# Recurrence layer: one dense v per step, key products over half the rows each, PSUM banks by chunk parity

## The chip, the cores and the metric
The kernel runs on one core of one Trainium2 chip. The metric is the device time of one execution in microseconds, the median of several runs. Engines are named as in the profile: PE is TensorE, ACT ScalarE, DVE VectorE, POOL GpSimd, SP the queue that issues most transfers.

## The reference
Two layers of a backbone over 256 latent and 256 context tokens of width 1024. Layer 0 is a state-space layer, layer 1 a chunked gated delta rule, and each is followed by an MLP. The change lies in the recurrence of layer 1: 16 heads, head dimension 128, chunks of 64 tokens, two directions, first over the four chunks of the context and then over the four of the latents. For every chunk and direction it computes

```python
v_new = u_i - einsum('bhcd,bhde->bhce', w_i, state)
new_state = state * exp(glast_i)[..., None, None] + einsum('bhcd,bhce->bhde', kend_i, v_new)
o_i = einsum('bhcd,bhde->bhce', qg_i, state) + einsum('bhcs,bhse->bhce', intra_i, v_new)
```

`u_i` and `w_i` come from a triangular inverse of a 64 x 64 matrix per chunk, head and direction. The outputs of the latents are normalised per head, gated, and multiplied by `w_out`.

## The kernel before
All projections, the MLPs and the readout are products of weights and activations that are split in a high and a low part, three products each. The recurrence layer runs in `gdn_phase` as a set of tasks: projections (`gdn_proj`, tile `proj`), convolutions (`conv_silu`), inverses (`gdn_t`, tiles `ap`, `up`, `ep`, `wp`), chains (`gdn_chain`), normalisation (`gdn_read`, `ot`) and the product with `w_out` (`gdn_out`, `wo`). `drive` steps through the tasks with a clock of its own, `Clock`, which estimates each instruction; the order of the program follows from it and from the scheduler of the tile framework. Each engine then runs its instructions in the fixed order, waiting on semaphores.

A chain is one head. Its two directions run side by side in one tile: at step n direction 0 works on chunk n and direction 1 on chunk 3-n or 11-n. The two chunks have different parity, so one has partitions 0 to 63 and the other 64 to 127 (`rows`). Eight steps make a chain, and at most NCH = 3 chains run at a time, in slots x = 0, 1, 2. A step consists of
- `ks`: keys x state, one product of 128 rows and 64 columns of the array per direction (in the profile `c<-S,kt`)
- `r0` on VectorE: values minus decay times `ks` (`r<-c,neg,vs`)
- `ub`: the inverse x `r0`, one 64 x 64 product per direction, written over `ks` (`c<-r,ub`, in the first step `c<-vs,ub`)
- `v2` on ScalarE: that product scaled per token (`v<-c,vsc`); from step 4 on also `vn`, its plain copy (`vn<-c`), and before it `qs`, queries x state
- `kv`: `v2` x keys (`c<-v,kn`), then the new state `S` on VectorE, one instruction per direction
- from step 4 on `op`: intra-chunk weights x `vn`, added to the output `oa`

Before, `v2` is two blocks of 128 columns, one per direction. In each block the other direction's 64 rows stay at the zeros that `gdn_zero` wrote once, so one full-array product gives both states:

```python
for d in range(2):
    nc.scalar.activation(v2[rows[d], d], vp[rows[d]], AF.Identity, scale=...)
kvw = self.cb[x][:, 128:384]
mm(kvw, kn[:, ms], v2.rearrange("p d e -> p (d e)"))
```

Each chain has a PSUM bank of its own, `cb[x]` (tiles `c0`, `c1`, `c2`): `ks` in columns 0 to 127 and the two states in 128 to 383.

Of the kernel before, what the change touches and what calls it, by code (L numbers as in the profile page):

```python
# [8 lines left out]
F32 = mybir.dt.float32  # L9
# [3 lines left out]
AF = mybir.ActivationFunctionType  # L13
# [1407 lines left out]
NPR, NT, NQK, NCH, NHI, NRB, LZ = 1, 2, 4, 3, 2, 3, 2  # L1421
# [36 lines left out]
class K3(K2):  # L1458
# [3 lines left out]
    def gdn_init(self, pool):  # L1462

        nc, V, G = self.nc, self.nc.vector, self.nc.gpsimd
        P = self.g = pool
        c2 = self.c2 = P.tile([128, NCONST2], F32, name="c2")
        nc.sync.dma_start(c2, self.I["consts2"])
        self.cw = P.tile([128, 32, 5], F32, name="cw")
        nc.sync.dma_start(self.cw, self.I["conv"])
        self.onh = P.tile([128, 1], F32, name="on")  # L1470
        nc.sync.dma_start(self.onh, self.I["onorm"])
        self.pp, self.npp = [], 0
        for n in range(2):
            t = P.tile([128, 524], F32, name=f"pp{n}")
            self.pin(G.memset(t, 0.0))
            self.pp.append(t)
        self.id16 = P.tile([128, 64], F16, name="id16")
        self.pin(G.tensor_copy(self.id16, c2[:, M_ID:M_ID + 64]))
        self.idm2 = P.tile([128, 128], F16, name="idm2")
        self.pin(G.tensor_scalar(self.idm2, self.ident, -2.0, None, op0=OP.mult))  # L1480
        self.id1k = P.tile([128, 64], F32, name="id1k")
        self.pin(G.tensor_scalar(self.id1k, c2[:, M_ID:M_ID + 64], 1024.0, None, op0=OP.mult))
        V.tensor_scalar(self.cw, self.cw, 0.5, None, op0=OP.mult)
        V.tensor_scalar(self.onh, self.onh, 0.5, None, op0=OP.mult)
        self.nb, self.lo = [], []
        for n in range(2):
            for L, name in ((self.nb, "nb"), (self.lo, "lo")):
                L.append(P.tile([128, 8, 128], F16, name=f"{name}{n}"))
        self.cb = [self.bank(f"c{n}", f"c{n}", bufs=1) for n in range(3)]

        self.cp = [(b[:, 0:128], b[:, 128:256], b[:, 256:384]) for b in self.cb] + [tuple(b[:, 384:512] for b in self.cb)]
        self.nhi, self.loeng = NHI, (G, V)
        self.wslot, self.hslot, self.wq = Slots(4), Slots(NHI), []
        self.cslot, self.fslot = Slots(2), Slots(2)
        self.pslots, self.nproj = [Slots(NPR), Slots(1)], 0
        self.oslot = [Slots(1) for _ in range(NCH)]
        self.v2 = []
        for x in range(NCH):
            self.v2.append([P.tile([128, 2, 128], F32, name=f"v2{x}{n}") for n in range(2)])

    def swapped(self, x, h, d, n):

# [334 lines left out]
    def gdn_chain(self, p, h2, st):  # L1837

        nc, V = self.nc, self.nc.vector
        W = self.gw  # L1840
        kt, qt, kn, vs = st["kt"], st["qt"], st["kn"], st["vs", h2]
        x = (2 * p + h2) % NCH
        ks, *kv = self.cp[x]
        vp = ks
        hd = 2 * p + h2
        col = lambda x, n: x[:, n, hd:hd + 1]
        new = lambda name, shape, bufs=1: W.tile(shape, F32, name=f"{name}{x}", bufs=bufs)
        mm = lambda o, l, r: nc.tensor.matmul(o, l, r, start=True, stop=True, skip_group_check=True)
        S = None
        for n in range(8):  # L1850
            cs = (n, 3 - n if n < 4 else 11 - n)
            rows = [slice(64 * (c % 2), 64 * (c % 2) + 64) for c in cs]
            ms, lat = MS[n], n >= 4
            if S is None:
                r0 = vs[:, ms]
            else:
                for d in range(2):
                    mm(ks[rows[d]], kt[:, cs[d]], S[:, d])
                r0 = new("r0", [128, 128])
                V.scalar_tensor_tensor(r0, ks, col(self.neg, n), vs[:, ms], op0=OP.mult, op1=OP.add)  # L1860
                if lat:
                    qs = self.tr("qs")[:, 0:128]
                    for d in range(2):
                        mm(qs[rows[d]], qt[:, cs[d] - 4], S[:, d])
                yield
            for d in range(2):
                mm(vp[rows[d]], st["ub", d][rows[d], cs[d] // 2, h2], r0[rows[d]])
            if n < 7:
                v2 = self.v2[x][n % 2]
                for d in range(2):  # L1870
                    nc.scalar.activation(v2[rows[d], d], vp[rows[d]], AF.Identity, scale=self.vsc[rows[d], n, hd:hd + 1])
            if n == 4:
                yield from self.oslot[x].take()
                oacc = st["o", h2] = new("oa", [128, 2, 128])
            if lat:
                oa = oacc[:, ms - 2]
                if n < 6:
                    nc.scalar.activation(oa, qs, AF.Identity, scale=col(self.egs, n))
                else:
                    V.scalar_tensor_tensor(oa, qs, col(self.egs, n), oa, op0=OP.mult, op1=OP.add)  # L1880
                vn = new("vn", [128, 128])
                nc.scalar.copy(vn, vp)
            yield
            if n < 7:
                if x < 3:
                    kvw = self.cb[x][:, 128:384]
                    mm(kvw, kn[:, ms], v2.rearrange("p d e -> p (d e)"))
                else:
                    for d in range(2):
                        mm(kv[d], kn[:, ms], v2[:, d])  # L1890
                Sn = new("S", [128, 2, 128], 2)
                if S is None:
                    if x < 3:
                        nc.scalar.copy(Sn.rearrange("p d e -> p (d e)"), kvw)
                    else:
                        for d in range(2):
                            nc.scalar.copy(Sn[:, d], kv[d])
                else:
                    for d in range(2):
                        V.scalar_tensor_tensor(Sn[:, d], S[:, d], self.egl[:, n, d, hd:hd + 1], kv[d],  # L1900
                                               op0=OP.mult, op1=OP.add)
                S = Sn
                yield
            if lat:
                op = self.tr("op")[:, 0:128]
                for d in range(2):
                    mm(op[rows[d]], st["ibd", d][rows[d], cs[d] // 2 - 2, h2], vn[rows[d]])
                V.tensor_tensor(oa, oa, op, op=OP.add)
                yield
# [130 lines left out]

    def gdn_zero(self):

        for t in self.nb + self.lo + [t for v in self.v2 for t in v]:
            self.pin(self.nc.gpsimd.memset(t, 0.0))
            yield

# [215 lines left out]
```

## Time and profile before
| | us |
|---|---|
| runs | 1623.61, 1618.85, 1622.08 |
| median | 1622.08 |
| the profiled execution | 1624.46 |
| its span, first to last instruction | 1622.7 |

| engine | busy us | share | instructions |
|---|---|---|---|
| PE | 1469.8 | 91% | 12370 |
| DVE | 1096.8 | 68% | 2036 |
| ACT | 776.3 | 48% | 1635 |
| POOL | 650.6 | 40% | 590 |

TensorE's clock as granted is 0.947 of full over the span. The recurrence layer runs from about 755 to 1420 us: projections alone at first, chains from 900 us on, the last projection at 1332 us, the last chain's end at about 1397 us, and the rest of `w_out` after it. An fp32 product is two matmul records in the profile, so 224 records of `c<-v,kn` are 112 products.

### The profile page before, as it was taken

The numbers are of one execution on the slowest core, as the hardware profiler recorded it, in microseconds if no ns is written. First come the engines' busy times: TensorE is split into PE (matmuls) and PEld (weight loads), VectorE is DVE, ScalarE is ACT, GpSimd is POOL, SyncE is SP. The second block draws the span as 40 slices with busy tenths as digits, with TensorE's granted clock in tenths as the row PEclk, the third lists the DMA queues.
The fourth block names the chain that finished last, engine by engine and source line by source line (L and its number), as shares of the span: only waits on it lengthen the run. The fifth ranks groups of instructions, "written<-read, shape, count | busy, mean of one in ns | idle before, by whom it ended". The sixth has DMA issues, their size and how long they took to land. (4 is left out here: it accounts for less than half of the span.)

```text
span 1622.7 us, 31318 instructions
## 1 busy us (share of the span) xinstructions
PE 1469.8 (91%) x12370; PEld 1115.6 (69%) x12370; DVE 1096.8 (68%) x2036; ACT 776.3 (48%) x1635; POOL 650.6 (40%) x590
## 2 busy tenths in 40 slices
PE   6898558999999999997978898989998999989998
PEld 2355436777777788886767676767776665689997
DVE  6978858774334344447999967686978875667766
ACT  3243456553223232325556655656675755554543
POOL 3962003642333233334776734353544400024432
PEclk7999779998999999998979999989998999999999
DMA  9887743554455533322222211111111102536552
GB/s 274 290 270 250 110 91 132 173 192 146 139 173 178 177 118 104 104 78 81 93 66 66 66 53 60 40 60 44 56 63 57 41 25 96 196 121 198 181 193 91
DMA packets 76771, 200.77 MB, mean 124 GB/s; under 512 B 8784, under 2 KB 29008, under 8 KB 76368
## 3 DMA queue, kind: packets, MB, share of 16 engines
q1 hardware_dynamic: 76112, 197.78, 38.5%
q8 instruction: 97, 1.59, 0.4%
q10 hardware_dynamic: 512, 0.98, 0.3%
q14 instruction: 50, 0.41, 0.1%
HBM read 192.71 MB, written 6.03 MB: 122 GB/s over the span
## 5 line engine op out<-in xcount | busy, mean ns | idle before, releaser
L273 ACT CAST whi<-wraw 128x1024 fp32r<-128x1024 f32 x221 | 225.3, 1045 | 239.5 <-PE w L273 149.2
L273 POOL TENSOR_TENSOR wlo<-wraw,whi 128x256 fp32r<-128x256 f32 (+1 forms) x221 | 208.3, 970 | 289.5 <-ACT whi L273 271.9
L273 DVE TENSOR_TENSOR wlo<-wraw,whi 128x1024 fp32r<-128x1024 f32 (+1 forms) x189 | 225.1, 1220 | 61.7 <-ACT whi L273 60.3
L273 PE MATMUL w<-hh,whi 128*128 128x256 f32 (+1 forms) x512 | 169.9, 335 | 0.0
L273 PE MATMUL w<-hl,whi 128*128 128x256 f32 (+1 forms) x512 | 168.9, 331 | 0.0
L273 PE MATMUL w<-hh,wlo 128*128 128x256 f32 (+1 forms) x512 | 168.4, 331 | 0.4 <-DVE wlo L273 0.4
L273 PE MATMUL w<-whi,h1l 128*128 128x512 f32 x384 | 148.4, 390 | 0.0
L273 PE MATMUL w<-wlo,h1h 128*128 128x512 f32 x384 | 148.4, 389 | 0.0
L273 POOL TENSOR_TENSOR sq<-rl 128x512 f32<-128x512 f32 (+1 forms) x64 | 62.4, 975 | 213.7 <-ACT rl L273 213.7
L273 PE MATMUL w<-whi,h1h 128*128 128x512 f32 x384 | 147.7, 393 | 0.0
L273 PE MATMUL proj<-hh,whi 128*128 128x256 f32 (+1 forms) x360 | 132.4, 368 | 7.4 <-ACT pp L273 6.7
L273 DVE TENSOR_TENSOR ma<-w,g 128x512 f32<-128x512 f32 x96 | 65.3, 687 | 105.3 <-PE w L273 105.2
L273 PE MATMUL proj<-hh,wlo 128*128 128x256 f32 (+1 forms) x360 | 127.5, 354 | 1.3 <-POOL wlo L273 1.3
L273 PE MATMUL proj<-hl,whi 128*128 128x256 f32 (+1 forms) x360 | 127.5, 354 | 0.0
L273 DVE SCALAR_TENSOR_TENSOR cacc<-pp,cw,cacc 128x520 f32<-128x520 f32 (+1 forms) x128 | 112.4, 879 | 9.6 <-ACT cacc L273 8.1
L273 POOL TENSOR_TENSOR xr<-xr,ma 128x512 f32<-128x512 f32 x56 | 79.5, 1421 | 89.2 <-DVE ma L273 89.2
L273 DVE TENSOR_TENSOR h1l<-sq,h1h 128x512 fp32r<-128x512 f32 (+1 forms) x64 | 35.5, 555 | 114.4 <-POOL sq L273 111.9
L273 ACT ACTIVATE v<-c,vsc 64x128 f32<-64x128 f32 x224 | 80.7, 362 | 62.4 <-PE c L273 57.6
L273 PEld LDWEIGHTS w<-hh,whi 128*128 128x128 f32 x512 | 98.0, 192 | 14.9 <-DVE wlo L273 2.5
L273 PEld LDWEIGHTS w<-hl,whi 128*128 128x128 f32 x512 | 98.2, 192 | 10.7 <-issue 1.9
L273 PEld LDWEIGHTS w<-hh,wlo 128*128 128x128 f32 x512 | 97.9, 192 | 10.2 <-issue 0.8
L273 ACT ACTIVATE rl<-w 128x512 f32<-128x512 f32 (+1 forms) x64 | 31.3, 489 | 130.1 <-PE w L273 120.8
(316 smaller groups left out, 3480.2 us busy)
## 6 DMA issues: line engine op xcount, KB each, us to landing
wraw<-in_w_dram SPq DMA_DIRECT2D x128, 512.0 KB, 4.3
adaw<-in_ada_w_dram SPq DMA_DIRECT2D x92, 512.0 KB, 4.8
wraw<-in_w_in_dram SPq DMA_DIRECT2D x48, 512.0 KB, 3.2
wraw<-in_w_glu_dram SPq DMA_DIRECT2D x32, 512.0 KB, 3.3
wraw<-in_w_out_dram SPq DMA_DIRECT2D x16, 512.0 KB, 3.5
Kt<-kd SPq DMA_DIRECT2D x32, 128.0 KB, 6.2
X<-grd SPq DMA_DIRECT2D x32, 128.0 KB, 3.2
V<-in_ada_w_dram SPq DMA_DIRECT2D x4, 512.0 KB, 6.1
```

Source lines behind the costliest of these rows:

```text
L273: r = f(*args, **kw)
```

## The change
`v2` becomes one tile of 128 x 128 in which each direction has its own 64 rows, written by one ScalarE instruction. The product with the keys becomes two, each over the 64 rows of one direction and with all 128 columns of the array. Since the two run in different row halves, they write different banks. The banks are dealt out anew: `ks` of all three chains lies in `c2`, the state of the even chunk in `c0` and that of the odd chunk in `c1`, each chain in its own 128 columns. The copy of the first state becomes two instructions, and the clears of `v2` go.

```diff
-        self.cp = [(b[:, 0:128], b[:, 128:256], b[:, 256:384]) for b in self.cb] + [tuple(b[:, 384:512] for b in self.cb)]
+        self.cp = [tuple(self.cb[n][:, 128 * x:128 * x + 128] for n in (2, 0, 1)) for x in range(NCH)]
...
-            self.v2.append([P.tile([128, 2, 128], F32, name=f"v2{x}{n}") for n in range(2)])
+            self.v2.append([P.tile([128, 128], F32, name=f"v2{x}{n}") for n in range(2)])
...
-        ks, *kv = self.cp[x]
+        ks, *kvs = self.cp[x]
...
-                for d in range(2):
-                    nc.scalar.activation(v2[rows[d], d], vp[rows[d]], AF.Identity, scale=self.vsc[rows[d], n, hd:hd + 1])
+                nc.scalar.activation(v2, vp, AF.Identity, scale=col(self.vsc, n))
...
-                if x < 3:
-                    kvw = self.cb[x][:, 128:384]
-                    mm(kvw, kn[:, ms], v2.rearrange("p d e -> p (d e)"))
-                else:
-                    for d in range(2):
-                        mm(kv[d], kn[:, ms], v2[:, d])
+                kv = [kvs[c % 2] for c in cs]
+                for d in range(2):
+                    mm(kv[d], kn[rows[d], ms], v2[rows[d]])
                 Sn = new("S", [128, 2, 128], 2)
                 if S is None:
-                    if x < 3:
-                        nc.scalar.copy(Sn.rearrange("p d e -> p (d e)"), kvw)
-                    else:
-                        for d in range(2):
-                            nc.scalar.copy(Sn[:, d], kv[d])
+                    for d in range(2):
+                        nc.scalar.copy(Sn[:, d], kv[d])
...
-        for t in self.nb + self.lo + [t for v in self.v2 for t in v]:
+        for t in self.nb + self.lo:
```

The order of the recurrence layer changes as a whole, because the planner's clock sees other instructions and other banks. Three places show how. In the rows a name's digits after the letter are the chain's slot (`S0`, `r01`, `v210` belong to slots 0, 1 and 1), the number behind the underscore is the tile's own, and the engine behind `waits` is that of the semaphore.

TensorE between the last projection and the first product of `wo`, before: `ks` of the chains in slots 0, 2 and 1.

```order
L273 MATMUL c0_6466<-S0_15218,kt_12408 64x128 [waits DVE_49]
L273 MATMUL c0_6466<-S0_15218,kt_12408 64x128
L273 MATMUL c2_6468<-S2_15456,kt_13768 64x128 [waits Activation_49]
L273 MATMUL c2_6468<-S2_15456,kt_13768 64x128
L273 MATMUL c1_6467<-S1_15127,kt_12408 64x128 [waits DVE_49]
L273 MATMUL c1_6467<-S1_15127,kt_12408 64x128
```

The same engine in the same part of the program now: steps of slots 0 and 1, one after the other.

```order
L273 MATMUL c2_6468<-r00_15082,ub0_13973 64x128 [waits DVE_49]
L273 MATMUL c2_6468<-r00_15082,ub1_14615 64x128
L273 MATMUL c1_6467<-v201_6470,kn_12444 128x128 [waits Activation_49]
L273 MATMUL c0_6466<-v201_6470,kn_12444 128x128
L273 MATMUL c2_6468<-S1_15102,kt_12580 64x128 [waits Activation_49]
L273 MATMUL c2_6468<-S1_15102,kt_12580 64x128
L273 MATMUL op_15148<-vn0_15109,ibd0_13172 64x128 [waits DVE_49]
L273 MATMUL op_15148<-vn0_15109,ibd1_13682 64x128
```

Before, the `ks` products of three slots stood next to each other, each in its own bank; now `kv` of slot 0 stands right behind its own `ub`, and the `ks` of slot 1 waits for ScalarE, which reads slot 0's columns of `c2`.

TensorE a little earlier in that part, now: the two products of one `kv` (of `v201`) with a `ks` of the other slot between and behind them.

```order
L273 MATMUL c0_6466<-v201_6470,kn_12444 128x128 [waits DVE_49,Activation_49]
L273 MATMUL c2_6468<-S1_14933,kt_12580 64x128
L273 MATMUL c1_6467<-v201_6470,kn_12444 128x128 [waits DVE_49]
L273 MATMUL c2_6468<-S1_14933,kt_12580 64x128
L273 MATMUL qs_14984<-S0_14944,qt_12684 64x128 [waits DVE_49]
```

Before, a `kv` was one product, as here with its neighbours in the same part:

```order
L273 MATMUL c0_6466<-v200_6469,kn_12226 128x256 [waits Activation_49]
L273 MATMUL c2_6468<-v220_6473,kn_13631 128x256 [waits Activation_49]
L273 MATMUL c1_6467<-v211_6472,kn_12226 128x256 [waits Activation_49]
L273 MATMUL op_15155<-vn1_15120,ibd0_13117 64x128 [waits PE_49]
L273 MATMUL op_15155<-vn1_15120,ibd1_13798 64x128
```

The two halves are instructions of their own now, and other products stand between them.

VectorE in the same part, before: `r0` of three slots in a row, with waits for TensorE, and one for ScalarE behind a first state.

```order
L273 SCALAR_TENSOR_TENSOR r00_15248<-c0_6466,neg_7014,vs0_12711 128x128 [waits PE_49]
L273 SCALAR_TENSOR_TENSOR r02_15463<-c2_6468,neg_7014,vs0_14051 128x128 [waits PE_49,Activation_49]
L273 SCALAR_TENSOR_TENSOR r01_15179<-c1_6467,neg_7014,vs1_12954 128x128 [waits PE_49]
L273 SCALAR_TENSOR_TENSOR oa1_15011<-qs_15181,egs_7002,oa1_15011 128x128 [waits DVE_49,PE_49]
L273 TENSOR_TENSOR oa0_15003<-oa0_15003,op_15227 128x128 [waits DVE_49,PE_49]
```

VectorE now:

```order
L273 SCALAR_TENSOR_TENSOR r01_14978<-c2_6468,neg_7008,vs1_13152 128x128 [waits DVE_49,PE_49,Activation_49]
L273 SCALAR_TENSOR_TENSOR r00_14982<-c2_6468,neg_7008,vs0_12881 128x128 [waits DVE_49,PE_49]
L273 SCALAR_TENSOR_TENSOR S1_15031<-S1_14933,egl_6992,c1_6467 128x128 [waits DVE_49,PE_49]
L273 SCALAR_TENSOR_TENSOR S1_15031<-S1_14933,egl_6992,c0_6466 128x128 [waits PE_49]
L273 SCALAR_TENSOR_TENSOR S0_15055<-S0_14944,egl_6992,c1_6467 128x128 [waits PE_49]
```

Every `r0` reads `c2` now, and the two states of a chain come from `c0` and `c1`, each with a wait of its own.

## Rows read from the trace of the kernel before

**Rows 1.** Stretches: us, busy us (instructions) by engine, granted clock, DMA share, GB/s

```profile
core 0: us, PE busy (x) PEld busy (x) DVE busy (x) ACT busy (x) POOL busy (x), PEclk, DMA share, GB/s
...
900.00:1331.00 431.00, 401.09 (x4943) 293.73 (x4943) 332.34 (x734) 268.17 (x705) 185.22 (x197) 0.96 0.16 51
1331.00:1350.00 19.00, 16.71 (x182) 10.92 (x182) 10.25 (x34) 10.98 (x35) 2.79 (x4) 1.00 0.28 98
1350.00:1397.00 47.00, 44.87 (x273) 27.60 (x273) 26.99 (x74) 24.58 (x63) 1.71 (x2) 1.00 0.33 111
```

**Rows 2.** Whom TensorE waited for, 900 to 1397: us, times, longest

```profile
PE c L273 <- DVE S L273: 9.5, 8, 4.8
PE ap L273 <- DVE T L273: 5.2, 4, 4.5
...
PE c L273 <- DVE r L273: 3.8, 4, 2.6
PE c L273 <- ACT vn L273: 3.3, 6, 1.1
PE c L273 <- ACT v L273: 3.1, 7, 0.7
```

**Rows 3.** Stretches again, around one of the dips of the clock

```profile
1220.00:1237.00 17.00, 12.22 (x105) 9.26 (x102) 13.69 (x25) 7.18 (x14) 10.40 (x9) 0.70 0.23 68
```

**Rows 4.** Instructions of tile v: count, ns min/median/max, first and last start

```profile
L273 ACT ACTIVATE v<-c,vsc x224: 343/363/382, 911.6 to 1385.6; 64x128 f32<-64x128 f32 x112
...
L273 PE MATMUL c<-v,kn x224: 377/379/796, 913.8 to 1388.6; 128*128 128x256 f32 x112
```

**Rows 5.** TensorE in order of time, 1340 to 1351: start, us, instruction, records

```profile
1341.74 0.82 PE L273 MATMUL c<-S,kt 128*64 128x128 f32 x12
1342.39 0.39 PE L273 MATMUL qs<-S,qt 128*64 128x128 f32 x4
...
1342.98 0.82 PE L273 MATMUL c<-r,ub 64*64 64x128 f32 x12
1343.78 0.43 PE L273 MATMUL c<-vs,ub 64*64 64x128 f32 x4
1344.83 0.70 PE L273 MATMUL c<-v,kn 128*128 128x256 f32 x2 [0.62 <-ACT v L273]
...
1346.75 0.44 PE L273 MATMUL qs<-S,qt 128*64 128x128 f32 x4
1347.12 0.70 PE L273 MATMUL c<-v,kn 128*128 128x256 f32 x2
1347.74 0.66 PE L273 MATMUL c<-S,kt 128*64 128x128 f32 x8
```

**Rows 6.** All engines in the same stretch, in order of time

```profile
1342.23 0.86 DVE L273 SCALAR_TENSOR_TENSOR r<-c,neg,vs 128x128 f32<-128x128 f32 x3
...
1343.46 0.27 ACT L273 COPY vn<-c 128x128 f32<-128x128 f32 x1 [2.66 <-PE c L273]
...
1348.23 0.61 DVE L273 SCALAR_TENSOR_TENSOR r<-c,neg,vs 128x128 f32<-128x128 f32 x2 [0.65 <-PE c L273]
```

**Rows 7.** TensorE in order of time, 1373 to 1377

```profile
1374.01 0.59 PE L273 MATMUL c<-v,kn 128*128 128x256 f32 x2
1374.26 0.58 PE L273 MATMUL wo<-wlo,oh 128*128 128x512 f32 x1
1374.68 0.39 PE L273 MATMUL wo<-whi,ol 128*128 128x512 f32 x1
1374.91 0.59 PE L273 MATMUL c<-v,kn 128*128 128x256 f32 x2
1375.43 0.43 PE L273 MATMUL op<-vn,ibd 64*64 64x128 f32 x4
```

## Prediction
> **What bounds the kernel now.** I read the profile in this order: the busy table by stretch, then who waits for whom on TensorE, then TensorE's order of time where the change falls. [rows 1] TensorE is the busiest engine of the recurrence: 401.1 of 431 us from 900 to 1331 us, 44.9 of 47 from 1350 to 1397, with ScalarE at 268.2 and 24.6 in the same stretches. After 1420 us the program is the last MLP, which the change doesn't touch, and before 755 us nothing of it runs. So time there is what TensorE does, plus what it idles. [rows 2] gives its idling from 900 to 1397: the long waits are for VectorE (S 9.5 us in 8, r 3.8 in 4, T 5.2 in 4), those for ScalarE are small (vn 3.3 in 6, v 3.1 in 7). [rows 3] shows what the longest of them bring: after a wait for r, the granted clock averages 0.70 over 17 us, so 5 us of full clock are lost behind a wait of 2.6 us. There are four such dips from 900 to 1331, and the mean of 0.96 there [rows 1] is 17 us of full clock. The change takes nothing from VectorE and adds nothing to it, so I treat where they fall as an accident of the order.
>
> **ScalarE's part.** Two half-height instructions a step become one: 224 of 363 ns [rows 4] become 112, 40.7 us of ScalarE. The first step of each of the 16 chains now copies two states apart instead of both in one, which gives back at most a copy of 0.27 (vn, [rows 6]) each, 4 us; six clears of v fall off GpSimd. TensorE's work on other chains, projections and inverses covers ScalarE here: it waits only 3.1 us for v. What the saving can give at most is that and the 3.3 for vn; what the copies can cost uncovered is their 4. I count nothing, because the wait for vn moves: today the product kv waits for vn, although it reads nothing of vn and shares only the bank; tomorrow kv has other banks, and the next product into ks, of whichever chain, waits there instead.
>
> **TensorE's own work.** The 112 products v x keys are full-array today. [rows 5] 1347.12 to 1347.74: 0.62 us with small-tile products on both sides; [rows 7] 1374.91 to 1375.43: 0.52 with a full-array one ahead; 1374.01 to 1374.68 holds one kv and one wo, and a wo alone takes 0.23 (1374.68 to 1374.91), so 0.44 between full-array ones. By their neighbours in the order that is 40 x 0.62 + 34 x 0.52 + 19 x 0.44 + 8 x 0.53 + 11 x 0.5 = 61 us. In the new order the 224 half products stand in 129 stretches, since 38 stand alone, cut off from their partner by a product of another shape, and 40 of the stretches follow a full-array product and add a change of shape, 0.10 (0.62 less 0.52). The trace has no pair with 64 rows and 128 columns. The nearest row is a lone pair of small tiles, 0.37 (1346.75 to 1347.12, weights half as wide); the bound above is a pair that doesn't overlap at all, today's 0.62. I take 0.42, near the lower since a second pair beside the first costs only 0.22 (1341.74 to 1342.39: three in 0.65), which is overlap of the same kind: 129 x 0.42 + 40 x 0.10 = 58 us. So 3 us are saved; with the bounds, 9 saved or 23 lost.
>
> The Trainium skill, "TensorE: Matmul & The Clock Gate", Part 3 (packing small matmuls), gives 3.07x for four row tiles at once. By an estimate from that page a pair would take 0.44 / 1.5 = 0.29 us plus the change of shape, and the saving would be nearer the 9; no row here shows row tiles side by side.
>
> **What the banks do.** All three chains now write ks into the bank c2 and share c0 and c1 for the two states. In the order with its waits, 189 TensorE instructions of a chain wait for another chain's read of a c tile, and 79 on ScalarE and VectorE; before, none do. That such a wait is made without any shared data is what [rows 2] shows with kv and vn.
>
> The Trainium skill, "PSUM — Partial Sum Buffer", section "PSUM bank collisions raise a hardware error", has two engines kept apart by bank and 32-partition quadrant, whatever the columns. By that rule the chains can't read and write c2 at once, because r, v and vn span all 128 partitions; the trace agrees (3.3 us in six waits).
>
> What this costs is seen at the end. Today three chains run abreast: three ks pairs in 0.65, their three r, 0.86 together [rows 6], three ub pairs in 0.80 [rows 5]. In the new order, after the last projection, ks of one chain waits for r of the other, and ub for the other's v, so they come one at a time; and kv stands directly behind its own ub. Counted in the order: kv with at most two matmuls between it and its own ub, 2 of 112 before, 27 now; ub so close behind its ks, 2 before, 22 now. A close kv: ub at 1343.78, kv at 1344.83 with 0.62 of waiting for v [rows 5], less one of the two halves of v (0.36), leaves 0.28. A close ub: ks to r is 0.49 (1347.74 to 1348.23 [rows 5, 6]), of which a lone pair is 0.44 (1346.75) and the hop 0.05; r takes 0.30 (two in 0.61 [rows 6]), and the hop back is taken as long, so 0.84 less the 0.37 after which TensorE is free again: 0.47. After the last projection there are 15 more close kv and 9 more close ub: 15 x 0.28 + 9 x 0.47 = 8.4 us. Nothing can hide that: no projection is left, and w_out's products start, in the order, only after 17 of the remaining 26 steps (8 of 19 before). Before the last projection it is 10 x 0.28 + 11 x 0.47 = 8.0; there TensorE already idles for a late VectorE, which catches up while TensorE waits, so I take half, 4, with 0 and 8 as ends.
>
> **Queues behind the waits.** TensorE takes its instructions in the order shown, so behind a waiting kv or ks stand op, qs and the products of the inverses. On VectorE the r of one chain waits for the other's v on ScalarE (51 waits), and behind it stand the state updates, the convolutions and the inverse's masks; ScalarE has 28 such, with the casts of the weights behind them. SP issues the same loads, and the clears that go stand before the first chain.
>
> **Sum.** Against the profiled execution's 1624.5 us (span 1622.7): -3 + 8.4 + 4 = +9.4, so 1634. The median of the runs is 1622.1, 2.4 below that execution; against the median it is 1632, 0.6% slower.
>
> **Rivals.**
> *Faster.* The halves overlap as the best rows (-9), and the waits for v and vn go without coming back elsewhere (-6.4); the closeness costs nothing as VectorE's lateness takes it up: 1622 - 15 = 1607. For it: ScalarE is relieved by 40 us and is itself waited for; against: 27 and 22 close pairs, most of them where nothing else is left to run.
> *No change.* The 3 us saved and half of the closeness cancel, or a dip like [rows 3] less (2.6 + 5 = 8 us) pays for it: 1620 to 1626.
> *Much slower.* Halves don't overlap: 129 x 0.62 + 4 = 84 us, +23, with the 12.4 of waits 1622 + 36 = 1658. It decides at about 0.55 us a pair; against it speaks the 0.22 of column tiles side by side, for it that no row tiles are seen.
> *It doesn't do what it says.* If ScalarE's one v took as long as two (726 ns), the close kv would each cost 0.64: 27 x 0.36 = 10 us more, 1642. Against it: ScalarE's copy vn of 128 partitions x 128 columns takes 0.27 [rows 6], less than one half of v, so I give it little.
>
> **Numbers.** Forecast 0.45, faster 0.20, no change 0.22, much slower (with the last one) 0.13. About 0.3%, 5 us, is what a measurement of this kernel can tell from no change; the forecast's own range, 1627 to 1641, lies above that. So faster 0.20, same 0.22, slower 0.58. One dip more or less shifts every case by 8 us. The range 1608 to 1655 takes in most of all four and leaves out the far ends of the first and the third.
>
> **What would show it.** v: 112 rows of about 0.36 us on ScalarE. Right: a kv pair alone from its start to the next product in 0.37 to 0.5 us; wrong if near 0.62. Between the last projection and the first w_out product some 40 us instead of 19 [rows 1] (17 steps at today's 2 us each, and most of the 8.4), with TensorE's busy share below today's 0.88 and waits of c for r, v and vn in its list; wrong if that stretch is as dense as now. Waits of r for v, and of v for r, in the lists of VectorE and ScalarE. A granted clock from 900 to 1331 other than 0.96 would say that the dips moved, and the total is then off by that. The forecast is wrong as a whole if TensorE's waits for c products don't rise by some 10 us.

## The result, and the profile after

The changed kernel takes 1734.5 us (median of four runs, 1731.7 to 1736.3) against 1622.8 (1618.9 to 1625.4): a ratio of 1.069, 95% interval 1.066 to 1.072. The forecast had the sign right; the loss is 112 us where it said 10, and the time lies above its range of 1608 to 1655. The profiled execution has a span of 1734.5 us. Ahead of the first chain and in the last MLP the traces agree, so the loss lies in the recurrence.

Stretches before, cut at the last projection, the first and the last product with w_out; columns as in [rows 1].

```profile
900.00:1332.00 432.00, 402.09 (x4950) 294.73 (x4951) 332.60 (x734) 269.04 (x708) 185.22 (x197) 0.96 0.16 51
1332.00:1350.00 18.00, 15.71 (x174) 9.92 (x174) 9.99 (x33) 10.11 (x32) 2.79 (x4) 1.00 0.29 103
1350.00:1422.50 72.50, 70.02 (x385) 48.02 (x386) 45.02 (x108) 38.21 (x86) 2.40 (x3) 1.00 0.46 152
```

The same three stretches after, and two more: the one of [rows 1], and the longest dip before the last projection, to set beside [rows 3].

```profile
900.00:1385.50 485.50, 426.83 (x5076) 316.19 (x5075) 334.16 (x714) 231.05 (x617) 190.45 (x201) 0.91 0.14 47
1385.50:1449.00 63.50, 51.25 (x296) 28.09 (x294) 20.06 (x61) 13.85 (x47) 3.79 (x5) 0.53 0.10 33
1449.00:1533.30 84.30, 82.25 (x381) 51.53 (x380) 44.03 (x101) 31.37 (x65) 1.39 (x2) 0.85 0.38 127
...
900.00:1331.00 431.00, 379.60 (x4436) 280.90 (x4435) 300.14 (x635) 208.06 (x552) 174.71 (x186) 0.92 0.14 48
...
1270.00:1305.00 35.00, 29.81 (x425) 22.05 (x424) 26.70 (x59) 15.54 (x38) 12.04 (x11) 0.71 0.09 31
```

Length less PE's busy time is idle time. The granted clock says the rest: it has two levels, 2.4 and 1.2 GHz. From the trace's clock records I summed the time at half clock and PE's busy time in it. Half of that busy time stands in the table as the cost of the half clock. It is an upper figure, since a small-tile pair goes from 0.37 to 0.62 us (below), which is a loss of 40% and not 50. Nor is it what the program would gain at full clock, since an engine that works faster may only wait longer. All in us:

| stretch | length before, after | idle before, after | at half clock before, after | cost of the half clock before, after |
|---|---|---|---|---|
| 900 to last projection | 432.1, 485.6 | 29.9, 58.7 | 34.1, 92.2 | 13.4, 42.3 |
| to first w_out product | 18.1, 63.4 | 2.3, 12.3 | 0, 59.6 | 0, 24.2 |
| to last w_out product | 72.3, 84.3 | 2.5, 2.1 | 0, 25.7 | 0, 12.6 |
| all | 522.5, 633.3 | 34.7, 73.0 | 34.1, 177.5 | 13.4, 79.2 |

So of 111 us, 38 are idle time, 53 to 66 the half clock (at 40 or 50% of the busy time in it), and the rest, 7 to 20, is more time of products. This is book-keeping; what causes what is for the runs to say. TensorE's waits from 900 to 1497, to set beside [rows 2]:

```profile
PE c L273 <- ACT v L273: 16.4, 32, 1.0
PE c L273 <- DVE r L273: 12.3, 20, 4.3
PE proj L273 <- DVE zs L273: 7.6, 5, 2.3
PE c L273 <- DVE S L273: 5.9, 7, 1.6
...
PE c L273 <- ACT vn L273: 0.8, 2, 0.4
```

Waits for v and r come to 28.7 us in 52, against 6.9 in 11 [rows 2]. What they look like is seen behind the last projection. TensorE in order of time, in the changed kernel:

```profile
1389.36 0.78 PE L273 MATMUL c<-v,kn 64*128 64x128 f32 x4 [0.47 <-ACT v L273]
1390.07 0.69 PE L273 MATMUL c<-S,kt 128*64 128x128 f32 x4
1391.28 0.70 PE L273 MATMUL c<-S,kt 128*64 128x128 f32 x4 [0.52 <-DVE r L273]
1392.43 0.69 PE L273 MATMUL c<-r,ub 64*64 64x128 f32 x4 [0.45 <-DVE r L273]
1393.64 0.69 PE L273 MATMUL c<-r,ub 64*64 64x128 f32 x4 [0.52 <-ACT v L273]
1394.26 0.80 PE L273 MATMUL c<-v,kn 64*128 64x128 f32 x4
...
1409.53 0.69 PE L273 MATMUL c<-S,kt 128*64 128x128 f32 x4
1410.15 0.69 PE L273 MATMUL op<-vn,ibd 64*64 64x128 f32 x4
1410.78 0.69 PE L273 MATMUL qs<-S,qt 128*64 128x128 f32 x4
1411.40 0.69 PE L273 MATMUL c<-r,ub 64*64 64x128 f32 x4
1412.56 0.80 PE L273 MATMUL c<-v,kn 64*128 64x128 f32 x4 [0.47 <-ACT v L273]
1413.29 0.69 PE L273 MATMUL c<-S,kt 128*64 128x128 f32 x4
```

The second ks (1391.28) reads nothing of r; it waits until VectorE has read the first chain's ks out of the same bank. The second ub (1393.64) waits for the other chain's v in the same way. Where [rows 5] shows three ks pairs at once in 0.65 us, they now come one by one. From 1409 to 1423 a fixed cycle runs, five pairs a chain step, 3.76 us from one ks to the next (1409.53 to 1413.29), all at half clock.

By the Trainium skill, "PSUM — Partial Sum Buffer", section "PSUM bank collisions raise a hardware error", a program has to guard accesses of different engines by bank and quadrant and not by address. The trace shows such a guard: the wait of 0.52 at 1391.28 lies between two chains with no column in common.

v itself is as forecast. Its row, to set beside [rows 4], and the halves of kv:

```profile
L273 PE MATMUL c<-v,kn x448: 272/373/580, 915.0 to 1496.9; 64*128 64x128 f32 x150
L273 ACT ACTIVATE v<-c,vsc x112: 346/368/403, 908.2 to 1496.3; 128x128 f32<-128x128 f32 x112
```

### The profile page after: what moved, and what is told of

Its sections match the earlier page's. It is cut to its first block, busy times and chain, and to the rows that moved or that the text cites. A ratio compares the mean times of both kernels' runs of the same rounds, so it can differ in the third digit from the quotient of the medians.

```text
span 1734.5 us, 31767 instructions
## 1 busy us (share of the span) xinstructions
PE 1539.5 (89%) x12594; PEld 1156.2 (67%) x12594; DVE 1103.3 (64%) x2036; ACT 736.0 (42%) x1539; POOL 649.9 (37%) x584
## 5 line engine op out<-in xcount | busy, mean ns | idle before, releaser
L273 POOL TENSOR_TENSOR rstd<-ms,mhalf 128x1 f32<-128x1 f32 (+2 forms) x22 | 17.4, 790 | 295.3 <-DVE ms L273 295.3
L273 DVE SCALAR_TENSOR_TENSOR S<-S,egl,c 128x128 f32<-128x128 f32 x192 | 59.4, 340 | 90.2 <-PE c L273 89.5
```

Of the source, the lines that this page charges most:

```text
L273: r = f(*args, **kw)
```

## The experiments

Three theories. B: the shared banks make the loss, with the clock falling because TensorE waits. C: the clock falls because the key product no longer fills the array. D: the planner's order was unlucky. All runs compare with the kernel before on the same chip (1621.6 to 1623.7 us). "Half clock" below is its cost from 900 us to the last w_out product, "idle" PE's idle time there, both worked out as in the table above, from the one profiled execution of each kernel. The clock differs between executions of one kernel. Every execution has its mean granted clock on record, and one minus that clock, times the span, is the full-clock time that it lost over the whole program: 147 to 160 us in the four of the changed kernel, 92 to 127 in the four with rotated banks (below), 66 to 92 (mean 78) in 42 of the kernel before. So differences of half clock between kernels need more than one execution each.

**The banks alone, with v and kv of before.** Against the changed kernel:

```diff
-nc.scalar.activation(v2, vp, AF.Identity, scale=col(self.vsc, n))
+for d in range(2):
+    nc.scalar.activation(v2[rows[d], d], vp[rows[d]], AF.Identity, scale=...)
...
-    mm(kv[d], kn[rows[d], ms], v2[rows[d]])
+    mm(kv[d], kn[:, ms], v2[:, d])
```

> The new dealing of PSUM banks alone: v is again two blocks with zeros in two ScalarE instructions, and each state's product with the keys uses all 128 rows (two products of 128 columns). In its order 196 TensorE instructions of a chain wait for another chain's read of a c tile (189 in the changed kernel, 0 before). If the shared banks make the loss (theory B), nothing is gained back: about 1735 us, TensorE's waits for c products near the changed kernel's 36 us from 900 to 1533. If the loss is TensorE's clock, which falls because the product with the keys no longer uses the full array (theory C), the stretches at half clock after 900 us, 177 us in all in the changed kernel and 34 before, shrink to below 80, and what they cost (half of 177 less 34, some 70 us) comes back: about 1665 us. If the sharing costs no more than forecast (some 10 us): 1630 to 1640.

Measured: 1745.5 us, ratio 1.075 [1.071, 1.079]; idle 75.5, half clock 70.3. The whole loss is there without dense v and without half-row products, with 157 us at half clock where theory C asked for less than 80. Its waits are those of the changed kernel (columns as in [rows 2]):

```profile
PE c L273 <- ACT v L273: 16.7, 29, 1.3
PE ap L273 <- DVE T L273: 12.1, 13, 3.5
PE c L273 <- DVE r L273: 9.6, 17, 2.3
```

**The dense v alone, in the chains' own banks.** Against the kernel before; `kz` holds the keys twice, zero in the other half of the rows. Not shown in the cut: `v2` has one buffer per chain instead of two, and `kn` one instead of four.

```diff
-mm(kvw, kn[:, ms], v2.rearrange("p d e -> p (d e)"))
+for d in range(2):
+    mm(kv[d], st["kz"][:, cs[d] % 2, ms], v2)
...
+kz = st["kz"] = W.tile([128, 2, 4, 128], F32, name="kz", bufs=NQK)
+for d in range(2):
+    nc.gpsimd.tensor_scalar(kz[:, d]..., kn..., self.half[:, d:d + 1], None, op0=OP.mult)
```

> The other part of the change alone: v is one dense tile written by one ScalarE instruction, and the three chains keep their own banks. So that both states can go into one bank, the keys stand twice, each copy with zeros in the other half of the rows (GpSimd makes the copies, 16 instructions of 512 columns), and a state is a product of all 128 rows with 128 columns. ScalarE loses 40 us, nothing is shared. By the forecast's step on ScalarE (off the path, nothing gained) 1618 to 1626 us; by its rival, in which relief of ScalarE is felt, down to 1610. A loss of over 10 us would say that the dense v itself costs.

Measured: 1626.0 us, ratio 1.001 [0.999, 1.003]; idle 26.2, half clock 10.1. Half the instructions for v, and nothing won or lost (what the single buffer of `v2` takes from the gain, if anything, no run shows):

```profile
L273 ACT ACTIVATE v<-c,vsc x112: 344/367/415, 915.3 to 1386.2; 128x128 f32<-128x128 f32 x112
L273 POOL TENSOR_SCALAR kz<-kn,half x16: 1563/1721/2592, 814.8 to 1272.7; 128x512 f32<-128x512 f32 x16
```

**No full-array product, in own banks.** Against the kernel before:

```diff
-mm(kvw, kn[:, ms], v2.rearrange("p d e -> p (d e)"))
+for d in range(2):
+    half = slice(64 * d, 64 * d + 64)
+    mm(kvw[half], kn[:, ms][:, half], v2.rearrange("p d e -> p (d e)"))
```

> The kernel before with one thing changed: the product of v with the keys of the first three chains is split into two halves of 64 output rows (128 rows x 64 columns of the array each, 256 columns long), side by side like the products of ks. Banks, v and all waits are as before, and nothing is shared. Theory B: no loss beyond some microseconds of extra instructions, 1618 to 1632 us. Theory C: the full-array product is gone, so the half-clock stretches after 900 us grow from 34 us to over 80, and the time rises to 1645 us or more.

Measured: 1630.7 us, ratio 1.005 [1.003, 1.007]; idle 29.1, half clock 13.2, as before. Theory C in this form falls: column halves, which keep all 128 rows, leave the half clock where it was.

**Rotated banks.** Against the changed kernel, so that no two chains' ks share a bank:

```diff
-self.cp = [tuple(self.cb[n][...] for n in (2, 0, 1)) for x in range(NCH)]
+self.cp = [tuple(self.cb[n][...] for n in (x, (x + 1) % 3, (x + 2) % 3)) for x in range(NCH)]
```

> The changed kernel with the banks rotated: chain x has ks in bank x and its two states in the other two banks, so no two chains share the bank that r, v and vn are read from, though a bank still holds one chain's ks and two others' states. Waits of VectorE for another chain's ScalarE read fall from 51 to 6, of TensorE for ScalarE from 86 to 55; those of TensorE for VectorE stay (103 to 106). Theory B: about half of the loss comes back, 1680 us or less. Theory C: the products are the same small tiles, so the clock falls as before and the time stays within 1715 to 1745 us.

Measured: 1691.6 us, ratio 1.041 [1.037, 1.045]; idle 48.5, half clock 55.3. 43 us come back, where theory B said 55 or more and theory C 20 or less. The chains go abreast again; TensorE in order of time, behind the last projection, has ks of two chains half a microsecond apart, and their ub together:

```profile
1382.02 0.44 PE L273 MATMUL c<-S,kt 128*64 128x128 f32 x4 [0.36 <-DVE S L273]
...
1382.51 0.39 PE L273 MATMUL c<-S,kt 128*64 128x128 f32 x4
...
1383.05 0.82 PE L273 MATMUL c<-r,ub 64*64 64x128 f32 x8
```

**The smallest doses.** The kernel before with one tile of chain 0 in the free quarter of chain 2's bank, first ks, then one state:

```diff
+self.cp[0] = (self.cb[2][:, 384:512], *self.cp[0][1:])
```

> The kernel before with the smallest dose of sharing: only the ks of chain 0 moves, from its own bank into the free quarter of chain 2's bank. v, the product with the keys and chain 1 are as before. In its order 68 TensorE instructions of a chain wait for another chain's read of a c tile (0 before, 189 in the changed kernel) and 32 of ScalarE and VectorE (79 there). Theory B (the shared banks make the loss): by the number of waits about a third of the loss of the banks alone, 122 us in the run with the new dealing, so 1640 to 1665 us, with the time without products of TensorE up by 5 us or more and the half-clock stretches after 900 us over 60 us (34 before). The forecast's own prices (close kv 15 - 2 at 0.28, close ub 14 - 2 at 0.47) give 9 us: 1631. If only a bank that all three chains share costs anything: 1622.

Measured: 1687.3 us, ratio 1.039 [1.036, 1.042]; idle 72.2, half clock 31.1. One shared bank brings more than half of the loss, with as much idle time as in the changed kernel (72 and 73 us) and less than half of its half clock (31 and 79): more than the third that the number of waits gave, and seven times the forecast's own prices. Its waits:

```profile
PE c L273 <- ACT v L273: 18.5, 27, 1.7
PE ap L273 <- DVE T L273: 10.7, 9, 3.8
PE c L273 <- DVE r L273: 8.1, 15, 1.3
```

```diff
+self.cp[0] = (*self.cp[0][:2], self.cb[2][:, 384:512])
...
-                if x < 3:
+                if 0 < x < 3:
...
-                    if x < 3:
+                    if 0 < x < 3:
```

The last two make chain 0's product with the keys two of 128 columns, and the copy of its first state two instructions.

> The other small dose: the kernel before with one of chain 0's two states moved into the free quarter of chain 2's bank, ks and everything else in place; chain 0's product with the keys is two of 128 columns for it. In its order 33 TensorE instructions of a chain wait for another chain's read of a c tile (68 with one ks moved, 189 in the changed kernel). If each such wait costs alike (theory B by count): 64 us x 33 / 68 = 31, so about 1653 us. If what binds is a bank that holds ks, which r, v and vn read in turn in every step, and a state, written and read once a step, is harmless: 1618 to 1640 us, within what orders of one kernel differ by (38 us between the two orders of the kernel before).

Measured: 1654.0 us, ratio 1.019 [1.017, 1.022]; idle 42.3, half clock 21.9. The count of waits gave 1653, but the order alone can do as much, as the next runs show.

**How much is the order?** The planner's time grain changed and nothing else:

```diff
-def drive(clock, tasks, grain=0.25, until=None):
+def drive(clock, tasks, grain=0.3, until=None):
```

> The kernel before with the same work and waits in another order: the planner's time grain is 0.30 us instead of 0.25. It measures what an order alone is worth. If orders of the same work differ little, within 10 us of 1622. If the loss of the change is the luck of an order (theory D), orders of the same work differ by tens of us, and this one may be at 1640 or above.

> The changed kernel with the same work and waits in another order: the planner's time grain is 0.30 us instead of 0.25. Theory B: within 20 us of 1735, with the half-clock stretches after 900 us over 120 us. Theory D (luck of the order): it may land anywhere between 1625 and 1750; under 1690 would speak for D.

Measured: the kernel before 1659.6 us (ratio 1.022 [1.018, 1.026]; idle 47.3, half clock 21.7), the changed one 1733.6 (idle 75.5, half clock 71.8). The order is worth 37 us to the first and nothing to the second. A third order of the changed kernel comes from a planner that takes no notice of the sharing:

```diff
-lo, hi = self.region(ap) if eng != "tensor" else (0, 1 << 30)
+lo, hi = self.region(ap) if eng != "tensor" or str(getattr(ap.tensor, "tag", None)).split("_ps1")[0] in ("c0", "c1", "c2") else (0, 1 << 30)
```

> The changed kernel with a planner that isn't told that a product into a c tile waits for readers of other columns of it, so that it plans the chains as if each had banks of its own. The work is the same and so are the waits that the banks demand. If the loss comes from an order that the planner made poor by avoiding those waits: below 1690 us. If it comes from the waits themselves, which no order avoids (theory B): 1715 to 1760 us.

Measured: 1739.7 us, ratio 1.072 [1.069, 1.074]; idle 72.9, half clock 87.6. A second order (grain 0.30) for the doses:

> One ks shared, in another order (planner's grain 0.30 instead of 0.25); the first order gave 1687 us, the kernels without sharing 1622, 1626, 1631 and 1660. If sharing one ks costs: 1670 to 1710 us again. If that was the order: as likely 1625 to 1660.

> One state shared, in another order (grain 0.30); the first gave 1654 us, inside what the orders without sharing span (1622 to 1660). If the sharing of a state costs half of that of ks: 1645 to 1690. If it is harmless: 1620 to 1660, in which the order's part may be either way.

> Dense v with the chains' own banks, in another order (grain 0.30); the first gave 1626 us. The kernel before with this grain gave 1660, so 1620 to 1665 if only the order changes the time; over 1670 would say that a kernel without any sharing can lose as much as one with it.

> The rotated banks in another order (grain 0.30); the first gave 1692 us, 43 below the changed kernel. If it is the shared ks bank that this dealing relieves, 1670 to 1715 again; at 1730 or above the 43 us were the order.

| what chains share | first order: us, idle, half clock | second order |
|---|---|---|
| nothing (before) | 1622, 34.7, 13.4 | 1660, 47.3, 21.7 |
| nothing (dense v, own banks) | 1626, 26.2, 10.1 | 1630, 29.1, 19.7 |
| one state | 1654, 42.3, 21.9 | 1673, 48.9, 26.2 |
| one ks | 1687, 72.2, 31.1 | 1698, 69.1, 33.3 |
| all, rotated | 1692, 48.5, 55.3 | 1713, 57.7, 67.1 |
| all, ks in one bank (the change) | 1735, 73.0, 79.2 | 1734, 75.5, 71.8 |

Within each order the rank is the same but for the two kernels without sharing, so theory D falls for the change, for one ks and for the rotated banks. One state costs 13 to 43 us, according to the order and to which kernel without sharing it is set against; its size stays uncertain. Nor does the half clock follow the idle time: one ks has the idle time of the change at less than half of its half clock, in both orders (by all executions it loses 111 and 109 us of clock, the change 153 and 158).

**What half rows do.** The rotated dealing with full-array products, in both orders (edits as in the first run and in the rotation):

> The rotated banks with v and the key products of the kernel before (v in two blocks with zeros, products of all 128 rows); with half-row products this dealing gave 1692 us, 55 of them lost to the half clock after 900 us. If half rows let the clock fall: the half clock costs 35 us or less, and 1655 to 1680 us. If only the waits between the chains do: 50 us or more, and 1685 to 1715.

> The same in another order (grain 0.30), where half rows gave 1713 us and 67 lost to the half clock. If half rows let the clock fall: 45 us or less, and 1665 to 1695 us. If only the waits do: 55 us or more, and 1700 to 1730.

Measured: 1679.7 us (idle 53.4, half clock 26.6) and 1713.7 (idle 65.5, half clock 37.9). The clock is as the first theory said, the time of the second order as the other one said. In the profiled executions full rows take 29 us off the half clock in each order, and bring 5 and 8 us more idle time and 2 and 18 more of work. But these executions happen to lie far apart. By the clock of all executions, 4 with half rows and 2 with full ones in the first order and 2 and 2 in the second, the mean loss over the program is 110 against 97 us and 135 against 121, so 13 and 14 us; with ks in one bank it is 153 against 139 (the changed kernel and the run with the banks alone). Half rows lower the clock by some 13 us in three pairs of kernels, though single executions overlap in two of the three (92 to 127 and 90 to 104 in the first order). In time, full rows gain 12 us in the first order and nothing in the second, and with ks in one bank they lose 11. The stretch from 900 to 1480 us of the profiled execution with half rows (clock 0.90), columns as in [rows 1]:

```profile
900.00:1480.00 580.00, 531.53 (x5654) 379.95 (x5647) 390.01 (x851) 268.76 (x718) 193.87 (x206) 0.90 0.16 53
```

and with full ones, both in the first order (clock 0.95):

```profile
900.00:1480.00 580.00, 523.85 (x5707) 393.40 (x5707) 400.66 (x878) 322.41 (x841) 189.97 (x204) 0.95 0.19 61
```

**Does the half clock cost by itself?** First, idle work beside every kv of the changed kernel:

```diff
+for d in range(2):
+    nc.nc.tensor.matmul(self.cb[d][:, 384:512], kn[:, ms], v2, ...)
```

> The changed kernel with work added: behind each pair of half-row products, two full-array products of 128 columns (keys by v, all 128 rows) into the unused last quarter of the same two banks, which nothing reads. That is 224 products; before, one of 256 columns takes 0.44 us, so 0.22 each, 49 us more of TensorE at full clock. Theory B (shared banks, clock only follows the idling): nothing is won, so 1735 + 49 = about 1784 us, and the stretch between the last projection and the first output product stays near a granted clock of 0.53. Theory C (the clock falls for want of full-array work): the half-clock stretches go from 177 us to below 80, up to 70 us come back, so about 1715 us, below the changed kernel although it does more, and that stretch runs at over 0.8.

Measured: 1769.9 us, ratio 1.091 [1.089, 1.093], 35 more than the changed kernel, between the two theories; idle 59.5, half clock 55.2. Between the last projection and the first w_out product the clock averages 0.66 instead of 0.53. Then idle work in the last three chains alone:

```diff
+extra = lambda b: nc.nc.tensor.matmul(b[:, 128:384], kn[:, ms], S..., ...)
...
+    if hd > 12 and not lat:
+        extra(self.tr("xt"))
...
+    if hd > 12:
+        extra(qb)
...
+    if hd > 12 and S is not None:
+        extra(ob)
```

> The changed kernel with idle work in its last three chains alone: one full-array product of 256 columns (keys by state, read by nothing) behind each qs and each op, and in steps 1 to 3 behind ks, into columns of the t banks that nothing else uses. 34 products of 0.44 us, 15 us more at full clock. It asks what the half clock there costs by itself. If the clock falls because TensorE idles between the chains' small products, and the half clock then lengthens the chains (theory B with a feedback): the 85 us at half clock from 1389 shrink by 30 us or more, the stretch between the last projection and the first output product runs at over 0.65 instead of 0.53, and the time falls below the changed kernel's 1735, to 1710 to 1730, though it does more. If the half clock there costs nothing of its own (the chains wait for VectorE and ScalarE anyway): 1735 to 1750, with more products in the same wait.

Measured: 1753.3 us, ratio 1.079 [1.076, 1.083]. The clock didn't rise, so this run doesn't answer the question:

```profile
1396.00:1450.00 54.00, 48.53 (x212) 24.85 (x212) 13.20 (x41) 9.84 (x38) 1.01 (x1) 0.50 0.02 5
```

The same with three float16 products at each place:

```diff
-extra = lambda b: nc.nc.tensor.matmul(b[:, 128:384], kn[:, ms], S..., ...)
+extra = lambda b: [nc.nc.tensor.matmul(b[:, 128:512], self.nb[0][:, 0], self.nb[0][:, 0:3]..., ...) for _ in range(3)]
```

> As the run with idle work in the last three chains, but heavier in columns for the time they take: at each of the 34 places three float16 products of the full array, 384 columns long, in place of one float32 product of 256. At full clock they are 34 x 3 x 0.16 = 16 us and two changes of type each, some 0.1, 7 us: 23 us more. The float32 products did not lift the clock (92 us at half clock from 1391). If these hold it at full clock, the question of that run is asked again: the half clock costs by itself when the time is below the changed kernel's 1735 plus half of those 23 us, 1747 or less, with the stretch between the last projection and the first output product over 0.8; if the chains would wait for VectorE and ScalarE in any case, 1750 to 1760 in spite of the higher clock. If the clock stays at 0.5: 1765 to 1785, and the question stays open.

Measured: 1734.0 us, ratio 1.068 [1.065, 1.071]: as the changed kernel, with some 20 us of products more (34 places at 0.58 us each, half of what separates the two steps below). From the last projection to the first w_out product the clock averages 0.78 instead of 0.53, just short of the 0.8 that the expectation asked for. It is up in the middle:

```profile
1395.50:1415.50 20.00, 17.51 (x82) 9.25 (x82) 5.19 (x16) 2.88 (x9) 0.00 (x0) 0.50 0.06 22
1415.50:1443.00 27.50, 22.28 (x180) 11.61 (x178) 9.73 (x32) 7.95 (x31) 1.01 (x1) 1.00 0.03 11
1443.00:1452.00 9.00, 7.52 (x28) 3.92 (x28) 1.88 (x7) 0.73 (x2) 0.00 (x0) 0.50 0.00 0
```

One trace now shows the same chain step at both levels. TensorE in order of time, at 2.4 GHz and with no added product in this step:

```profile
1416.17 0.43 PE L273 MATMUL c<-r,ub 64*64 64x128 f32 x4
1417.07 0.49 PE L273 MATMUL c<-v,kn 64*128 64x128 f32 x4 [0.47 <-ACT v L273]
1417.49 0.44 PE L273 MATMUL c<-S,kt 128*64 128x128 f32 x4
1417.86 0.43 PE L273 MATMUL op<-vn,ibd 64*64 64x128 f32 x4
1418.23 0.46 PE L273 MATMUL qs<-S,qt 128*64 128x128 f32 x4
1418.62 0.44 PE L273 MATMUL c<-r,ub 64*64 64x128 f32 x4
```

From ub to ub 2.45 us, against 3.76 at 1.2 GHz in the changed kernel; the wait for v is 0.47 in both. So the half clock costs 1.31 us in a chain step of this kind by itself; for all 17 steps of the stretch that would be 22 us, an estimate. The step with the added products (1418.62 to 1422.23) takes 3.61, still under 3.76: with the clock up, more work took less time.

That holds where one step directly follows another. Over the whole program, time follows the clock loosely: with rotated banks the execution that lost 127 us of clock took 1698.4 us and the one that lost 92 took 1683.4, but in the third order of the changed kernel one that lost 168 took 1738.4 and one that lost 134 took 1741.1.

## Why the prediction was right or wrong

The cost of the shared banks is where the forecast failed: +12.4 us in the sum, 124 in the run with the banks alone (1745.5 against 1621.6). Two terms were wrong in it, the clock (set to nothing) and the idle time before the last projection (4 us).

- **ScalarE, 40.7 us off the path: right.** ScalarE's busy time falls from 776 to 736 us, and the run with dense v and own banks gains nothing (ratio 1.001).
- **The key product: right.** In the changed kernel's trace 58 pairs of halves at full clock with a product right behind them take 0.42 us (median), the value taken between 0.37 and 0.62. That row halves run side by side the runs show too: a half alone takes as long as a pair (with rotated banks, 1383.95 to 1384.37 and 1387.73 to 1388.15). What the forecast missed is that half rows also go with a lower clock, by some 13 us of lost clock; it priced them by time alone.
- **"An accident of the order" (the dips of the clock): the step that failed, and in the book-keeping the largest.** It was set to no change. The half clock cost 13.4 us before and 79.2 after, an upper figure. Without sharing, five kernels have 10 to 22; with all three banks shared (and no work added), eight have 27 to 88. What this is worth in time is shown for a chain step (1.31 us) and not for the whole. Before, each of the four dips begins in a wait of TensorE of 2.6 to 4.8 us or just behind one; this is the one of [rows 3]:

```profile
1225.50 0.43 PE L273 MATMUL c<-r,ub 64*64 64x128 f32 x4 [2.62 <-DVE r L273]
```

- Almost half of the time at half clock after is of another kind: one stretch from 1389 to 1475 us, 85 of 177. From the last projection's products to its start at the kv at 1389.36, shown above, no wait is longer than 0.52 us, and inside it no idle time is longer than 0.7; it ends among the products with w_out. So more long waits alone don't explain the clock.
- **Behind the last projection: the waits were sized about right.** Idle time from there to the last w_out product rises by 9.6 us (2.3 and 2.5 before, 12.3 and 2.1 after), against 8.4. The forecast's 40 us for the stretch of 17 steps would fit 2.45 us a step, 17 x 2.45 = 42; 63.4 were measured, at half clock. Only four of the 17 steps run in the fixed cycle of 3.76, so that 17 x 3.76 = 64 is partly luck. (In the close kv, 0.62 less 0.36 is 0.26 and not 0.28; that changes the sum by 0.3 us.)
- **Before the last projection: mis-sized.** The forecast took 4 us, at most 8, since VectorE "catches up while TensorE waits". Idle time rose by 28.8 there, apart from the clock. Only pairs that stand close in the order were counted. That a chain held up by another chain's read is late everywhere is the likely reason: TensorE's wait for the gates' zs goes from 0.6 to 7.6 us, VectorE's for the new states from 43.7 to 88.1. From 900 us on, before:

```profile
PE proj L273 <- DVE zs L273: 0.6, 1, 0.6
...
DVE S L273 <- PE c L273: 43.7, 34, 5.1
DVE r L273 <- PE c L273: 16.0, 22, 4.2
```

and after:

```profile
DVE S L273 <- PE c L273: 88.1, 59, 4.6
DVE r L273 <- PE c L273: 37.2, 39, 4.3
```

- **Waits up "by some 10 us": they rose by 19** (r, vn and v from 10.2 to 29.5).
- **The rivals.** "Much slower" (1658) rested on halves that don't overlap; they do. No rival had more of the clock in it than one dip of 8 us, though the text named the sign to look for: a clock from 900 to 1331 other than 0.96 (it is 0.92).

What stays open: why the clock falls as far as it does, and how much of the 112 us it costs. By the means of all executions the change loses 75 us of clock more than the kernel before, the banks alone 61, and the other 14 come with half rows; idle time alone doesn't predict it. No run has half rows without shared banks. None of these kernels is faster than the one before; the best, dense v in own banks, measures the same.

## What to carry to other kernels

Where a small buffer is kept apart by bank, sharing a bank between independent chains couples them: one ks moved into a neighbour's bank cost 38 to 65 us here against the kernel before in the same order. Price such a change by what a chain that runs late does to everything behind it, and not by the pairs that stand close in the order. And when a change adds waits to TensorE, put a term for the clock into the sum: in the book-keeping here it was larger than the idle time (53 to 66 us against 38).

## What the hardware showed

- PE's busy share doesn't tell the clock. The changed kernel is 83% busy from 1400 to 1450 us (41.3 of 50) at 1.2 GHz, and the float16 run 81% busy from 1415.5 to 1443 (22.3 of 27.5) at 2.4 GHz. The Trainium skill, "TensorE: Matmul & The Clock Gate", Part 1 (the HAM clock gate), ties the clock to how busy the engine has been; the profile's busy share alone doesn't give the level here, and the measurement decides. At 1.2 GHz the same products also count as busy for longer (0.62 us a pair against 0.37).
- Float32 products of the full array between the chains' steps left the clock at 1.2 GHz at 90% busy (48.5 of 54 us); with three float16 ones of 384 columns in each place it was at 2.4 GHz for 27 of some 57 us. Over the whole program the four executions with float32 ones lost 134 to 154 us of clock, those with float16 ones 123 to 139, the changed kernel 147 to 160.
- Two float32 products over 64 rows each and 128 columns of the array run side by side: 0.42 us for the pair, 0.41 for one alone (medians at full clock in the changed kernel's trace).
